# Splitting weights further ahead around the stage turns of a decoder trunk, with later normalized slices

## The chip, the cores and the metric

The program runs on one core of a Trainium2 chip. The metric is the device time of one execution in microseconds, from three executions of the kernel before (median, lowest, highest). The profile is of one execution of its own. The engines are TensorE (PE; its weight loads are PEld), VectorE (DVE), ScalarE (ACT), GpSimd (POOL) and SyncE (SP, which issues the weight loads from memory).

## The reference

Two layers over x of 256 tokens by 1024. Each layer is a half-step SwiGLU FFN, a parallel mixer of three causal parts over one input projection, and a second half-step FFN. Each of the three is followed by a residual add and a layer norm.

```python
def swiglu_half(x, w1, w3, w2):
    return 0.5 * ((jax.nn.silu(x @ w1) * (x @ w3)) @ w2)
...
for l in range(DEPTH):
    x = layer_norm(ALPHA * x + swiglu_half(x, ffn1_w1[l], ffn1_w3[l], ffn1_w2[l]), ln1_g[l], ln1_b[l])
    h = x @ w_in[l]
...
    mix = jnp.concatenate([out_a, out_b, out_c], axis=-1) @ w_out[l]
    x = layer_norm(ALPHA * x + mix, ln2_g[l], ln2_b[l])
    x = layer_norm(ALPHA * x + swiglu_half(x, ffn2_w1[l], ffn2_w3[l], ffn2_w2[l]), ln3_g[l], ln3_b[l])
```

out_a is a chunked spatial gating, out_b a gated DeltaNet with eight heads, out_c a gated linear attention with four. The FFN is 2816 wide.

## The kernel before, in words

**Precision by splitting.** x lies transposed in SBUF, features on partitions, as eight slices of 128 x 256. A product of f32 accuracy is three matmuls in fp32r (`mm3`, L224): each weight and each operand is split into a high half, rounded by ScalarE (L199, L232), and a low half, which VectorE gets by a subtraction (L200, L233). The three products are high by high, high by low, low by high.

**Units.** The weights are packed on the host into units of 128 x 1024 in the order in which they are used: `NU` = 167 a layer (66 for the first FFN, 35 for the mixer, 66 for the second FFN). `load` (L176) has SP fetch units into `NRAW` = 5 raw buffers, `conv` (L184) splits one unit into a pair wh, wl out of `NW` = 5 buffers and asks for a later load, and `done` (L212) runs when a unit has been used: it calls `conv` until `LOOK` = 2 further units stand split. A few units of the mixer (`WHOLE`) are used unsplit.

**Order.** The code is traced in program order. A scheduler at compile time then lays each engine's instructions into one fixed order, by priority among those whose inputs and buffers are ready in its own model. `ahead(n)` (L136) gives the instructions in it the priority of code n instructions earlier. At run time each engine follows its fixed order. `mx` tiles with one tag share one buffer, in turn.

**FFN.** `ffn` (L405) goes over 22 tiles of 128 hidden columns. Tile f takes a w1 and a w3 unit (24 matmuls each) into two PSUM banks h1 and h3, `epilogue` (L420) makes silu(h1) * h3 and splits it into gs, and two tiles later a w2 unit adds it into the four banks y that hold the FFN's output; the last two w2 units (four in the last FFN) come together at the end. In the last FFN the w2 product is taken with tokens on partitions, 512 columns per matmul, and tiles of x are transposed in between.

**The turn of a stage.** After an FFN or a mixer, `ln_open` (L327) adds the residual to y slice pair by slice pair (L338), multiplies by the norm's gain and splits the result into xH and xL (L341, L342), before mean and variance are known. The next stage's first matmuls run on this raw x; two extra columns (gain and bias, so 258 instead of 256) let the mean and the bias be put right afterwards: `raw_t` (L390) adds mean times the extra column (L394) and multiplies by 1/sigma (L395). Meanwhile GpSimd sums x over slices (L345 to L355), ScalarE squares it (L349), VectorE sums the squares (L351 to L356), two matmuls with a constant matrix (`ln_mm`, L358) give the means, and `ln_stats` (L363) makes 1/sigma in small steps on ScalarE and VectorE.

An FFN with a norm ahead of it (the second of layer 0, the first and the second of layer 1: three) computes its tiles 0 to 3 (`NORM` = 4) from raw x. Its statistics are traced between the two units of tile 1. Behind tile 1 the normalized x is made in place, `ln_d` and `ln_n` (L378, L382), alternately by VectorE and GpSimd, and behind tile 2 `ln_x` (L386) and eight splits make the pair x2 from which tiles 4 to 21 are computed. Tile 2 uses two of the y banks as h1 and h3. The mixer (L546) does the same with its first nine units; its three first (L647) run interleaved over the slices.

Of the kernel before, what the change touches and what calls it, by code (L numbers as in the profile page):

```python
# [25 lines left out]
KD = 8  # L26
DFF = 2816
XS = T + 8
NORM = 4
NF = DFF // P  # L30
NU = 2 * 3 * NF + 27 + 8
NRAW = 5
# [2 lines left out]
LAG = 2  # L35
PIECES = 1
FIRST = 3
HP0, HP1, HP2, HP7 = 0, 400, 300, 0
CONST = 3
EVAC = 12  # L40
CUTS = ((9, 1), (17, 4), (35, 4))
ORDER = "v0 sub cv a0 tk0 zz av v3 v1 l0a l0b z3 l1a v2 zr l1b tk1 avn tv z1 zm s0 cq s1 d1 d0 dk a1 c0 pp kt t0 sc s2 c1 t1 s3 c2 pz w1 po c3 t2 w3 t3 w0 w2".split()
# [81 lines left out]
def trunk(ctx: ExitStack, tc: tile.TileContext, xin, w_all, cin, pin, lin, gin, out, dbg=None, nlayers=L):  # L124
# [59 lines left out]
    def conv(upto):  # L184
        b = st["conv"]
        if b > min(upto, nunits - 1):
            return
        load(b)
        st["conv"] += 1
        if whole(b):  # L190
            load(b + NRAW + FIRST * (b < FIRST))
            return
        WH[b] = whp.tile([P, 1024], F32R, tag="wh", name=f"wh{b}")
        WL[b] = whp.tile([P, 1024], F32R, tag="wl", name=f"wl{b}")

        i = b % NU - 3 * NF
        w = 1024 // next((c for o, c in CUTS if 0 <= i < o), 1)
        for o in range(0, 1024, w):
            st["copy"] = A.copy(WH[b][:, o:o + w], raw[b][:, o:o + w])  # L199
            V.tensor_sub(WL[b][:, o:o + w], raw[b][:, o:o + w], WH[b][:, o:o + w].bitcast(F32))  # L200
# [11 lines left out]
    def done(b):  # L212
        for d in (WH, WL, raw):
            d.pop(b, None)
        while st["conv"] < nunits and (sum(not whole(u) for u in range(b + 1, st["conv"])) < LOOK):
            conv(st["conv"])

    def next_unit():
# [95 lines left out]
    def unit_tile(h, b, raw_in):  # L314
        w = T + 2 if raw_in else T
        for k in range(KD):
            mm(h, b, k, w)


# [7 lines left out]
    def ln_open(y, scale, l, n):  # L327
        gb = lnc(l, n)
        s2 = mx.tile([P, 2, T], F32, tag="Y", name="s2")
        q2 = mx.tile([P, 2, T], F32, tag="ls", name="q2")  # L330
        sums[:] = [s2, q2]
        with ahead(HP0):
            A.copy(xH[:, :, T:], gb)
            V.tensor_sub(xL[:, :, T:], gb, xH[:, :, T:].bitcast(F32))
            sqp = None
            for i in range(4):
                xs = x[:, 2 * i:2 * i + 2]
                V.scalar_tensor_tensor(xs, xs, scale, y[i].rearrange("p (a t) -> p a t", a=2),  # L338
                                       op0=ALU.mult, op1=ALU.add)
                for k in (2 * i, 2 * i + 1):  # L340
                    A.activation(xH[:, k, :T], x[:, k], AF.Copy, scale=gb[:, k, 0:1])  # L341
                    V.scalar_tensor_tensor(xL[:, k, :T], x[:, k], gb[:, k, 0:1], xH[:, k, :T].bitcast(F32),  # L342
                                           op0=ALU.mult, op1=ALU.subtract)
                if i == 1:
                    G.tensor_tensor(s2, x[:, 0:2], xs, op=ALU.add)  # L345
                elif i > 1:
                    G.tensor_tensor(s2, s2, xs, op=ALU.add)
                sq = wk.tile([P, 2, T], F32, tag="sq", name="sq")
                A.activation(sq, xs, AF.Square)  # L349
                if i == 1:  # L350
                    V.tensor_add(q2, sqp, sq)  # L351
                elif i > 1:
                    V.tensor_add(q2, q2, sq)
                sqp = sq
            G.tensor_tensor(s2[:, 0], s2[:, 0], s2[:, 1], op=ALU.add)  # L355
            V.tensor_add(q2[:, 0], q2[:, 0], q2[:, 1])  # L356

    def ln_mm(ps, which):  # L358
        with ahead(0):
            PE.matmul(ps[:, which * T:(which + 1) * T], lhsT=C("mean"), rhs=sums[which][:, 0],  # L360
                      start=which == 0, stop=True, skip_group_check=True)

    def ln_stats(ps, eps, hp=0):  # L363

        t0 = wk.tile([P, T], F32, tag="t1", name="rs0")
        t1 = wk.tile([P, T], F32, tag="t3", name="rs1")
        with ahead(hp):
# [8 lines left out]
            V.scalar_tensor_tensor(rs, t0, 1.5, rs, op0=ALU.add, op1=ALU.mult)  # L376
# [18 lines left out]
        V.tensor_mul(t, t, rs)  # L395
        return t

    def raw_silu(dst, p, tag="t1"):
        cc = wk.tile([P, 1], F32, tag="cc", name="cc")
        V.tensor_copy(cc, p[:, T + 1:T + 2])  # L400
        t = raw_t(p, tag)
        act(dst, t, AF.Silu, bias=cc)


    def ffn(ln=None, last=None):  # L405
# [14 lines left out]
        def epilogue(f):  # L420
            h1, h3 = hq.pop(f)
            s = wk.tile([P, T], F32, tag="s", name="s")
            g = wk.tile([P, T], F32, tag="g", name="g")
            if ln and f < NORM:
                raw_silu(s, h1)
                t3 = raw_t(h3, "t3")
                V.scalar_tensor_tensor(g, t3, h3[:, T + 1:T + 2], s, op0=ALU.add, op1=ALU.mult)
            else:
                act(s, h1[:, :T], AF.Silu)
                V.tensor_mul(g, s, h3[:, :T])  # L430
            gH, gL = gs[:, 0, f % 4], gs[:, 1, f % 4]
            split(gH, gL, g)
            gq[f] = (gH, gL)

        pst = early = None
        for f in range(NF + LAG):
            if f < NF:
                if ln and f == 2:
# [4 lines left out]
                if f == 0:  # L443
                    w = T + 2 if ln else T
                    hs = [h1, h3]
                    if st["unit"] == 0:
                        early = hbank("h1")
                        hs.append(early)
                    bs = [next_unit() for _ in hs]
                    for k in range(KD):  # L450
                        for h, b in zip(hs, bs):
                            mm(h, b, k, w)
                    for b in bs:
                        done(b)
                else:
                    if early is None:
                        b = next_unit()
                        if ln and f == NORM:

                            PE.matmul(h1, lhsT=WH[b][:, :P], rhs=gs[:, :, (f - 3) % 4], start=True, stop=True,  # L460
                                      skip_group_check=True)
                        unit_tile(h1, b, ln and f < NORM)
                        done(b)
                    early = None
                    if ln and f == 1:
                        pst = ybank(0, "pst")
                        ln_mm(pst, 0)
                        ln_mm(pst, 1)
                        ln_stats(pst, ln[2])
                    b = next_unit()  # L470
                    unit_tile(h3, b, ln and f < NORM)
                    done(b)
                if f == CONST and st["unit"] < NU // 9:

# [7 lines left out]
                    epilogue(0)  # L482
                if not (ln and f == 0):
                    epilogue(f)
                if ln and f == 1:
                    for i in range(4):
# [59 lines left out]
    def mixer(l, n_ln, eps):  # L546
# [107 lines left out]
        for _, b, _, _ in hd:  # L654
            done(b)
        pst = ybank(0, "pst")
        ln_mm(pst, 0)
        ln_mm(pst, 1)
        ln_stats(pst, eps, HP1)
        h, _, t, i = hd[0]  # L660
        with ahead(HP2):
            epi(t, i)(h)
# [639 lines left out]
```

## Time and profile before

| | |
|---|---|
| three executions | 1102.03 us median, 1096.82 to 1108.56 |
| profiled execution | 1108.28 us, span from first to last instruction 1106.5 us |
| mean granted TensorE clock | 0.973 of full speed |
| read from memory | 179.81 MB, 163 GB/s over the span |
| first FFN of layer 0 | about 5 to 189 us |
| mixer of layer 0 | about 189 to 353 us |
| second FFN of layer 0 | about 353 to 542 us (turn 1 at its start) |
| first FFN of layer 1 | about 542 to 736 us (turn 2) |
| mixer of layer 1 | about 736 to 905 us |
| second FFN of layer 1 | about 905 to 1098 us (turn 3) |

A group of the profile reads: line, engine, operation, out<-in, shape, count | busy time, mean duration in ns of one | idle time of the engine just before them, and what ended it. A window gives length, then busy time and count of each engine, the granted clock, the share of the DMA engines and GB/s. A timeline row gives start, duration, engine, line, operation, and in brackets the idle time before it. Durations of neighbours on one engine can overlap a little, and those of matmuls do so much (0.28 us each, one every 0.113 us).

### The profile page before, as it was taken

To read this page: it belongs to the slowest core of one execution; us is meant where nothing else is said; L and a number is where in the kernel's file an instruction comes from. 1 tells how busy PE (TensorE), PEld (TensorE's weight loads), DVE (VectorE), ACT (ScalarE), POOL (GpSimd) and SP (SyncE) were. 2 spreads that over 40 slices of the span, in tenths; PEclk is the share of its full clock that TensorE was granted. 3 is DMA by queue.
4 is the path that set the end of the run, shared out by engine and by line. 5 is a ranking of instruction groups with operands and counts; after the bars stand their busy time and mean duration, and the time that the engine had idled before them with its cause. 6 is when DMAs were issued, how large, how long until landed. Compare 5 with 4: busy or idle time off the path is not lost. (4 is left out here: it accounts for less than half of the span.)

```text
span 1106.5 us, 23698 instructions
## 1 busy us (share of the span) xinstructions
PE 1062.1 (96%) x9875; PEld 1012.5 (92%) x9875; DVE 753.9 (68%) x1262; ACT 600.4 (54%) x1063; POOL 78.6 (7%) x62
## 2 busy tenths in 40 slices
PE   8999999999999899999989999999989998999996
PEld 7999999987889899999889999999787897999995
DVE  4555556989867965555786555579896679655556
ACT  5444445777556744444664444468664567444442
POOL 0100001101002200000220000020000012000000
PEclk9999999999999999999989999999996999999999
DMA  8855554442323375555336656534331234655541
GB/s 275 303 194 193 193 198 161 153 135 77 116 78 123 138 244 191 192 195 198 140 118 225 193 195 198 195 136 162 124 114 62 97 115 154 229 195 191 191 165 39
DMA packets 51515, 182.38 MB, mean 165 GB/s; under 512 B 5840, under 2 KB 7376, under 8 KB 51280
## 3 DMA queue, kind: packets, MB, share of 16 engines
q1 hardware_dynamic: 50544, 177.23, 47.6%
q10 hardware_dynamic: 864, 3.64, 0.9%
q8 instruction: 77, 1.26, 0.4%
q14 instruction: 30, 0.25, 0.1%
HBM read 179.81 MB, written 1.05 MB: 163 GB/s over the span
## 5 line engine op out<-in xcount | busy, mean ns | idle before, releaser
L200 DVE TENSOR_TENSOR wl<-raw,wh 128x1024 fp32r<-128x1024 f32 (+1 forms) x455 | 413.8, 926 | 236.9 <-ACT wh L199 236.6
L199 ACT CAST wh<-raw 128x1024 fp32r<-128x1024 f32 (+1 forms) x455 | 353.2, 800 | 365.8 <-issue 183.1
L227 PE MATMUL h<-x,wh 128*128 128x256 f32 x864 | 238.7, 276 | 0.0
L228 PE MATMUL h<-x,wh 128*128 128x256 f32 x864 | 238.6, 276 | 0.0
L229 PE MATMUL h<-x,wl 128*128 128x256 f32 x864 | 238.6, 276 | 0.0
L228 PEld LDWEIGHTS h<-x,wh 128*128 128x128 f32 x864 | 162.2, 188 | 0.8
L227 PEld LDWEIGHTS h<-x,wh 128*128 128x128 f32 x864 | 162.2, 188 | 0.7
L229 PEld LDWEIGHTS h<-x,wl 128*128 128x128 f32 x864 | 162.2, 188 | 0.0
L227 PE MATMUL y<-gs,wh 128*128 128x256 f32 x528 | 147.0, 279 | 7.2 <-ACT gs L232 7.2
L228 PE MATMUL y<-gs,wh 128*128 128x256 f32 x528 | 147.2, 279 | 0.0
L229 PE MATMUL y<-gs,wl 128*128 128x256 f32 x528 | 147.1, 279 | 0.0
L228 PE MATMUL h<-xL,wh 128*128 128x256 f32 (+1 forms) x472 | 132.9, 282 | 2.3 <-DVE xL L342 2.1
L227 PE MATMUL h<-xH,wh 128*128 128x256 f32 (+1 forms) x472 | 134.0, 284 | 0.8 <-ACT wh L199 0.7
L229 PE MATMUL h<-xH,wl 128*128 128x256 f32 (+1 forms) x472 | 133.2, 282 | 0.5 <-DVE wl L200 0.5
L227 PEld LDWEIGHTS y<-gs,wh 128*128 128x128 f32 x528 | 100.1, 190 | 7.6 <-ACT gs L232 7.6
L228 PEld LDWEIGHTS y<-gs,wh 128*128 128x128 f32 x528 | 100.6, 191 | 0.0
L229 PEld LDWEIGHTS y<-gs,wl 128*128 128x128 f32 x528 | 100.5, 190 | 0.0
L228 PEld LDWEIGHTS h<-xL,wh 128*128 128x128 f32 x472 | 90.5, 192 | 3.2 <-DVE xL L342 2.9
L227 PEld LDWEIGHTS h<-xH,wh 128*128 128x128 f32 x472 | 90.6, 192 | 1.7 <-ACT wh L199 1.2
L229 PEld LDWEIGHTS h<-xH,wl 128*128 128x128 f32 x472 | 90.5, 192 | 1.0 <-DVE wl L200 0.9
L430 DVE TENSOR_TENSOR g<-s,h 128x256 f32<-128x256 f32 x76 | 32.0, 421 | 45.8 <-PE h L229 37.3
L345 POOL TENSOR_TENSOR s<-x 128x512 f32<-128x512 f32 x5 | 7.1, 1416 | 520.7 <-DVE x L338 520.7
(363 smaller groups left out, 1960.9 us busy)
## 6 DMA issues: line engine op xcount, KB each, us to landing
raw<-w_all SPq DMA_DIRECT2D x331, 512.0 KB, 3.7
raw<-w_all SPq DMA_DIRECT2D x12, 128.0 KB, 4.1
pl<-pin ACTq DMA_DIRECT2D x2, 730.5 KB, 7.2
cst<-cin ACTq DMA_DIRECT2D x1, 1026.0 KB, 8.6
x<-xin SPq DMA_DIRECT2D x4, 256.0 KB, 4.2
out<-xT SPq DMA_DIRECT2D x4, 256.0 KB, 2.0
Gb<-gin ACTq DMA_DIRECT2D x1, 512.0 KB, 3.5
Bb<-gin ACTq DMA_DIRECT2D x1, 512.0 KB, 4.0
```

The source lines that it names most:

```text
L199: st["copy"] = A.copy(WH[b][:, o:o + w], raw[b][:, o:o + w])
L200: V.tensor_sub(WL[b][:, o:o + w], raw[b][:, o:o + w], WH[b][:, o:o + w].bitcast(F32))
L227: PE.matmul(o, lhsT=wh, rhs=mh, start=first, stop=False, **kw)
L228: PE.matmul(o, lhsT=wh, rhs=ml, start=False, stop=False, **kw)
L229: PE.matmul(o, lhsT=wl, rhs=mh, start=False, stop=last, **kw)
L345: G.tensor_tensor(s2, x[:, 0:2], xs, op=ALU.add)
L430: V.tensor_mul(g, s, h3[:, :T])
```

## The change

- `done` keeps more than two units split ahead near the end of a stage: up to six (`LOOK` + 4), from 12 units before the turn on, in steps; ahead of a second FFN, which follows a mixer, in the steps of a table over the last eight units.
- For 29 units the pair of halves lies in `mx` buffers that the mixer uses otherwise (`SPARE`, four pairs), so nine pairs are to be had around a turn. The second FFN's first four units use them, elsewhere every second unit from seven before to five behind the turn.
- `NORM` goes from 4 to 7: tiles 0 to 6 are computed from raw x.
- `ln_open` is written out in a new order, runs with `ahead(400)` instead of `ahead(0)`, and sums x on VectorE instead of GpSimd. The statistics of both kinds of stage run with `ahead(400)` (the FFN's had 0), the squares' mean first; in the FFN they are traced in the middle of tile 1's second unit.
- `epilogue` runs with `ahead(200)`; it copies h3's extra column as it did h1's, so that both banks are free after `raw_t`; the copy into the high half must come before the next change of ScalarE's table.
- The normalized x is made in four slices behind tiles 2 to 5, each queued behind that tile's gate, all on VectorE and ScalarE.

```diff
-NORM = 4
+NORM = 7
-HP0, HP1, HP2, HP7 = 0, 400, 300, 0
+HP0, HP1, HP2, HP7 = 400, 400, 300, 0
+HPE = 200
+SPARE = (("U64", "qd"), ("kb", "kd"), ("vb", "XP"), ("XA", "AT"))
+STAGES = sorted(l * NU + o for l in range(L) for o in (0, 3 * NF, 3 * NF + 35))[1:]
...
+    spare = {s + i: SPARE[n % 4] for s in STAGES
+             for n, i in enumerate(range(4) if s % NU == 3 * NF + 35 else range(-7, 6, 2))}
...
-        WH[b] = whp.tile([P, 1024], F32R, tag="wh", name=f"wh{b}")
-        WL[b] = whp.tile([P, 1024], F32R, tag="wl", name=f"wl{b}")
+        if b in spare:
+            WH[b], WL[b] = (mx.tile([P, 1024], F32R, tag=t, name=f"w{t}{b}") for t in spare[b])
+        else:
+            WH[b] = whp.tile([P, 1024], F32R, tag="wh", name=f"wh{b}")
+            WL[b] = whp.tile([P, 1024], F32R, tag="wl", name=f"wl{b}")
...
-        while st["conv"] < nunits and (sum(not whole(u) for u in range(b + 1, st["conv"])) < LOOK):
+        left = next((s - b for s in STAGES if s > b), 99)
+        if (b + left) % NU == 3 * NF + 35:
+            look = LOOK + {8: 1, 7: 1, 6: 1, 5: 2, 4: 3, 3: 4}.get(left, 4 if left < 3 else 0)
+        else:
+            look = LOOK + min(4, max(0, (14 - left) // 2))
+        while st["conv"] < nunits and (sum(not whole(u) for u in range(b + 1, st["conv"])) < look):
             conv(st["conv"])
...
+        def add_x(i):
+            V.tensor_add(s2, x[:, 0:2] if i == 1 else s2, x[:, 2 * i:2 * i + 2])
...
+            z(0)
+            square(0)
+            low(0)
+            z(1)
+            square(1)
+            low(1, 2)
+            z(2)
+            square(2)
+            low(3, 4)
+            z(3)
+            add_q(1)
+            square(3)
+            low(5, 6, 7)
+            add_x(1)
+            add_q(2)
+            add_x(2)
+            add_q(3)
+            add_x(3)
             V.tensor_add(q2[:, 0], q2[:, 0], q2[:, 1])
+            V.tensor_add(s2[:, 0], s2[:, 0], s2[:, 1])
...
-            if ln and f < NORM:
-                raw_silu(s, h1)
-                t3 = raw_t(h3, "t3")
-                V.scalar_tensor_tensor(g, t3, h3[:, T + 1:T + 2], s, op0=ALU.add, op1=ALU.mult)
...
+            with ahead(HPE):
+                if ln and f < NORM:
+
+                    c1 = raw_bias(h1)
+                    t1 = raw_t(h1, "t1")
+                    act(s, t1, AF.Silu, bias=c1)
+                    c3 = raw_bias(h3)
+                    t3 = raw_t(h3, "t3")
+                    st["gate"] = V.scalar_tensor_tensor(g, t3, c3, s, op0=ALU.add, op1=ALU.mult)
...
+                tab["ops"].append(A.copy(gH, g))
+                V.tensor_sub(gL, g, gH.bitcast(F32))
...
-                    unit_tile(h3, b, ln and f < NORM)
+                    unit_tile(h3, b, ln and f < NORM, stats if ln and f == 1 else None)
...
-                if ln and f == 1:
-                    for i in range(4):
-                        ln_d(V if i % 2 else G, i)
-                        ln_n(V if i % 2 else G, i)
-                if ln and f == 2:
-                    for k in range(KD):
-                        ln_x(ln[0], ln[1], k)
-                        split(x2[0][:, k], x2[1][:, k], x[:, k])
+                i = f - NORM + 5
+                if ln and 0 <= i < 4:
+                    with tc.issue_after(st["gate"].ins):
+                        ln_d(V, i)
+                        ln_n(V, i)
+                        for k in (2 * i, 2 * i + 1):
+                            ln_x(ln[0], ln[1], k)
+                            split(x2[0][:, k], x2[1][:, k], x[:, k])
```

More of the change, by code (lines that the diff above doesn't have):

```diff
@@ L312, in mm, with unit_tile @@
             mm3(h[:, :w], b, k, oh[:, k, :w], ol[:, k, :w], k == 0, k == KD - 1)
-    def unit_tile(h, b, raw_in):
+    def unit_tile(h, b, raw_in, mid=None):
         w = T + 2 if raw_in else T
         for k in range(KD):
+            if mid and k == KD // 2:
+                mid()
             mm(h, b, k, w)
@@ L331, in ln_open, with z, square, low @@
         sums[:] = [s2, q2]
+        sq = [q2, None, None, None]
+        def z(i):
+            xs = x[:, 2 * i:2 * i + 2]
+            V.scalar_tensor_tensor(xs, xs, scale, y[i].rearrange("p (a t) -> p a t", a=2),
+                                   op0=ALU.mult, op1=ALU.add)
+            for k in (2 * i, 2 * i + 1):
+                A.activation(xH[:, k, :T], x[:, k], AF.Copy, scale=gb[:, k, 0:1])
+        def square(i):
+            if i:
+                sq[i] = wk.tile([P, 2, T], F32, tag="sq", name="sq")
+            A.activation(sq[i], x[:, 2 * i:2 * i + 2], AF.Square)
+        def low(*ks):
+            for k in ks:
+                V.scalar_tensor_tensor(xL[:, k, :T], x[:, k], gb[:, k, 0:1], xH[:, k, :T].bitcast(F32),
+                                       op0=ALU.mult, op1=ALU.subtract)
+        def add_x(i):
+            V.tensor_add(s2, x[:, 0:2] if i == 1 else s2, x[:, 2 * i:2 * i + 2])
+        def add_q(i):
+            V.tensor_add(q2, q2, sq[i])
         with ahead(HP0):
@@ L334, in ln_open, with ln_stats @@
             V.tensor_sub(xL[:, :, T:], gb, xH[:, :, T:].bitcast(F32))
-            sqp = None
-            for i in range(4):
[L337 to L355, printed above, removed]
+            z(0)
[16 more added lines that the diff above has]
+            add_x(3)
             V.tensor_add(q2[:, 0], q2[:, 0], q2[:, 1])
+            V.tensor_add(s2[:, 0], s2[:, 0], s2[:, 1])
     def ln_mm(ps, which):
-        with ahead(0):
+        with ahead(HP1):
             PE.matmul(ps[:, which * T:(which + 1) * T], lhsT=C("mean"), rhs=sums[which][:, 0],
-                      start=which == 0, stop=True, skip_group_check=True)
-    def ln_stats(ps, eps, hp=0):
+                      start=which == 1, stop=True, skip_group_check=True)
+    def ln_stats(ps, eps):
         t0 = wk.tile([P, T], F32, tag="t1", name="rs0")
         t1 = wk.tile([P, T], F32, tag="t3", name="rs1")
-        with ahead(hp):
+        with ahead(HP1):
             A.copy(muN, ps[:, :T])
@@ L396, in raw_t, with raw_bias @@
         return t
-    def raw_silu(dst, p, tag="t1"):
+    def raw_bias(p):
         cc = wk.tile([P, 1], F32, tag="cc", name="cc")
         V.tensor_copy(cc, p[:, T + 1:T + 2])
-        t = raw_t(p, tag)
-        act(dst, t, AF.Silu, bias=cc)
+        return cc
     def ffn(ln=None, last=None):
@@ L423, in epilogue, with stats @@
             g = wk.tile([P, T], F32, tag="g", name="g")
-            if ln and f < NORM:
-                raw_silu(s, h1)
-                t3 = raw_t(h3, "t3")
[L427 to L432, printed above, removed]
-            gq[f] = (gH, gL)
-        pst = early = None
+            with ahead(HPE):
[6 more added lines that the diff above has]
+                    st["gate"] = V.scalar_tensor_tensor(g, t3, c3, s, op0=ALU.add, op1=ALU.mult)
+                else:
+                    act(s, h1[:, :T], AF.Silu)
+                    V.tensor_mul(g, s, h3[:, :T])
+                gH, gL = gs[:, 0, f % 4], gs[:, 1, f % 4]
+                tab["ops"].append(A.copy(gH, g))
+                V.tensor_sub(gL, g, gH.bitcast(F32))
+            gq[f] = (gH, gL)
+        def stats():
+            pst = ybank(0, "pst")
+            ln_mm(pst, 1)
+            ln_mm(pst, 0)
+            ln_stats(pst, ln[2])
+        early = None
         for f in range(NF + LAG):
@@ L464, in ffn @@
                     early = None
-                    if ln and f == 1:
[L466 to L469, printed above, removed]
                     b = next_unit()
-                    unit_tile(h3, b, ln and f < NORM)
+                    unit_tile(h3, b, ln and f < NORM, stats if ln and f == 1 else None)
                     done(b)
@@ L484, in ffn @@
                     epilogue(f)
-                if ln and f == 1:
-                    for i in range(4):
-                        ln_d(V if i % 2 else G, i)
-                        ln_n(V if i % 2 else G, i)
-                if ln and f == 2:
-                    for k in range(KD):
-                        ln_x(ln[0], ln[1], k)
-                        split(x2[0][:, k], x2[1][:, k], x[:, k])
+                i = f - NORM + 5
[3 more added lines that the diff above has]
+                        ln_n(V, i)
+                        for k in (2 * i, 2 * i + 1):
+                            ln_x(ln[0], ln[1], k)
+                            split(x2[0][:, k], x2[1][:, k], x[:, k])
             if f >= LAG:
@@ L656, in mixer @@
         pst = ybank(0, "pst")
+        ln_mm(pst, 1)
         ln_mm(pst, 0)
-        ln_mm(pst, 1)
-        ln_stats(pst, eps, HP1)
+        ln_stats(pst, eps)
         h, _, t, i = hd[0]
```

## The prediction

> **Bound now.** I read the page's busy shares first, then the span cut into windows, then what TensorE waited for, and last the groups and the order of VectorE's work around one stage turn. In the page the number after the percent sign is the count of instructions.
>
> ```profile
> PE 1062.1 (96%) x9875; PEld 1012.5 (92%) x9875; DVE 753.9 (68%) x1262; ACT 600.4 (54%) x1063; POOL 78.6 (7%) x62
> ```
>
> TensorE is busy nearly throughout, so only what keeps its matmuls from following each other can be won. Busy time hides that: a slow matmul is busy too. So I count matmuls by window (each row: length, busy time and count per engine, granted clock, DMA share, GB/s).
>
> ```profile
> 353.00:385.00 32.00, 27.31 (x207) 26.56 (x206) 32.00 (x54) 23.47 (x42) 10.47 (x7) 0.95 0.38 132
> 542.00:584.00 42.00, 36.54 (x257) 35.28 (x256) 39.03 (x67) 27.60 (x50) 12.12 (x8) 0.88 0.30 104
> 905.00:946.00 41.00, 36.33 (x259) 34.09 (x258) 40.70 (x67) 28.77 (x48) 10.29 (x7) 0.96 0.45 147
> 385.00:540.00 155.00, 155.00 (x1367) 154.96 (x1366) 89.25 (x106) 73.21 (x98) 0.00 (x0) 1.00 0.59 201
> 189.00:240.00 51.00, 49.83 (x430) 45.74 (x428) 48.60 (x105) 39.13 (x95) 4.94 (x3) 1.00 0.44 145
> 240.00:353.00 113.00, 107.04 (x1466) 94.55 (x1466) 87.66 (x215) 67.73 (x155) 12.90 (x12) 0.94 0.29 97
> 400.00:520.00 120.00, 120.00 (x1061) 120.00 (x1060) 65.29 (x74) 55.03 (x74) 0.00 (x0) 1.00 0.58 195
> 560.02:565.78 5.76, 5.76 (x50) 5.76 (x49) 5.76 (x9) 4.08 (x5) 2.67 (x2) 1.00 0.22 78
> ...
> L521 PE MATMUL y<-wh,gs 128*128 128x512 f32 x8 | 3.8, 474 | 0.0
> ```
>
> In the middle of an FFN (400 to 520) a 256-wide matmul goes by every 120/1061 = 0.113 us, and VectorE is busy little over half the time. A 258-wide matmul of a raw tile takes 5.76/48 = 0.120 (two units of 24; the row's 50 counts a neighbour at each edge). The first three rows are the three FFNs that open on a raw input. Charged wholly at the dearer 0.120, turn 1 needs 207 x 0.120 = 24.8 of its 32 us: 7.2 lost. Turn 2: 257 x 0.120 = 30.8 of 42: 11.2 lost. Turn 3 holds 24 matmuls with 512 columns (three lines like the last row, eight each), charged twice 0.113: 235 x 0.120 + 24 x 0.227 = 33.6 of 41: 7.4 lost. Together 25.8 us, all with VectorE at 93 to 100%.
>
> ```profile
> PE y L227 <- ACT gs L232: 7.2, 2, 4.1
> ...
> PE y L520 <- ACT gs L232: 4.1, 1, 4.1
> PE h L228 <- DVE xL L342: 2.1, 1, 2.1
> ...
> PE pmisc L228 <- DVE xL L342: 1.9, 2, 1.0
> ```
>
> TensorE's waits (total, times, longest) name the same places: the first w2 unit waits for the gated product of tile 0 once in each turn, 11.3 us, and the openings wait for the low halves of x. The 113 us of the mixer's middle are a chain of small steps; the change does not touch its steps.
>
> **VectorE's lateness.** These are its groups, two of GpSimd's, and single instructions, from the second turn.
>
> ```profile
> L200 DVE TENSOR_TENSOR wl<-raw,wh 128x1024 fp32r<-128x1024 f32 x11 | 13.4, 1218 | 2.0 <-ACT wh L199 2.0
> L342 DVE SCALAR_TENSOR_TENSOR xL<-x,lnp,xH 128x256 fp32r<-128x256 f32 x8 | 7.1, 921 | 0.0
> L395 DVE TENSOR_TENSOR t<-t,rs 128x256 f32<-128x256 f32 x8 | 5.3, 688 | 0.0
> L233 DVE TENSOR_TENSOR x<-x,x 128x256 fp32r<-128x256 f32 x8 | 3.1, 421 | 0.0
> L394 DVE SCALAR_TENSOR_TENSOR t<-muN,h 128x256 f32<-128x256 f32 x6 | 2.9, 477 | 1.2 <-PE h L229 1.2
> L380 DVE TENSOR_TENSOR x<-x,muN 128x512 f32<-128x512 f32 x2 | 2.4, 1224 | 0.0
> L427 DVE SCALAR_TENSOR_TENSOR g<-t,h,s 128x256 f32<-128x256 f32 x3 | 1.4, 481 | 0.0
> L400 DVE COPY cc<-h 128x1 f32<-128x1 f32 x3 | 0.5, 154 | 0.9 <-PE h L229 0.9
> ...
> L347 POOL TENSOR_TENSOR s<-s,x 128x512 f32<-128x512 f32 x2 | 4.1, 2032 | 3.5 <-DVE x L338 3.5
> L384 POOL TENSOR_TENSOR x<-x,rs 128x512 f32<-128x512 f32 x2 | 3.6, 1800 | 3.1 <-DVE rs L376 3.1
> ...
> 543.44 1.38 POOL L347 TENSOR_TENSOR s<-s,x 128x512 f32<-128x512 f32 x1 [1.05 <-DVE x L338]
> 543.58 1.51 DVE L342 SCALAR_TENSOR_TENSOR xL<-x,lnp,xH 128x256 fp32r<-128x256 f32 x1
> 545.02 0.68 DVE L351 TENSOR_TENSOR q<-sq 128x512 f32<-128x512 f32 x1
> 545.62 0.87 DVE L342 SCALAR_TENSOR_TENSOR xL<-x,lnp,xH 128x256 fp32r<-128x256 f32 x2
> 546.42 0.67 DVE L338 SCALAR_TENSOR_TENSOR x<-x,y 128x512 f32<-128x512 f32 x1
> 547.01 1.21 DVE L200 TENSOR_TENSOR wl<-raw,wh 128x1024 fp32r<-128x1024 f32 x1
> 548.15 0.68 DVE L353 TENSOR_TENSOR q<-q,sq 128x512 f32<-128x512 f32 x1
> ```
>
> Two things are to be seen. Splits of weights stand between the steps of the normalization. And the same L342 takes 1.51 us beside a GpSimd add and 0.40 (two in 0.80) without one. I also read from these starts that VectorE begins its next instruction about 0.08 us before the last one's end: L338 passes in 0.59, a split in 1.14.
>
> **The parts.**
>
> Two more windows are needed here: the busiest of a turn for the loads, and the mixer's last matmuls.
>
> ```profile
> 367.00:372.75 5.75, 5.75 (x51) 5.75 (x49) 5.75 (x10) 4.12 (x5) 2.65 (x3) 1.00 0.74 280
> 340.00:353.00 13.00, 13.00 (x113) 13.00 (x112) 8.35 (x14) 5.60 (x13) 4.85 (x6) 1.00 0.45 165
> ```
>
> *Splits ahead.* Four more units per turn are split before it: 4 x 1.14 = 4.6 us of VectorE leave each turn. Ahead of turn 2 and of both mixers they fall into the FFN's end, with VectorE idle 42% of the row 385 to 540. Twelve units instead of eight are then split in the last 22 us, 12 x 1.14 + 2.7 tiles x 0.7 = 15.6 us of VectorE: hidden. Their loads come earlier on SP's queue: 12 x 0.524 MB (128x1024 f32) in 22 us would be 286 GB/s, about the 280 that the first of the two windows moved, and five raw units are loaded in advance.
>
> Ahead of turns 1 and 3 they fall into the mixer's last matmuls: 13.0 - 8.35 = 4.7 us idle on VectorE there, against 4.6 wanted. It just fits; where it does not, a split is put into the mixer's last chain. I take 1.5 us lost for both layers (bounds 0, and four splits in the chain of each, 9).
>
> *The opening (five times).* GpSimd's sums move to VectorE: three adds at 0.60 and one at 0.34, +2.1. In return the eight L342 go from 7.1 to 8 x 0.40 = 3.2. Net -1.8 each. And it is placed ahead of the splits, so TensorE's first k-slices find their halves. By the wait rows that is 2.1 in turn 2 (inside the 25.8) and 1.9 at the mixers. The mixer's first 51 us show VectorE at 95% with TensorE nearly full, so freeing VectorE earns little more there: I take 2.5 for both mixers (bounds -3, and 5).
>
> *Statistics.* Both column sums need the opening's adds. VectorE's work after the last y bank is 0.59 + 3 x 0.40 + 6 x 0.60 + 2 x 0.34 = 6.1 us; the mean matmuls now stand in the middle of tile 1's second unit, 48 x 0.120 + 36 x 0.120 = 10.1 us after the turn. They wait for nothing. The means are four f32 matmuls, counted at 0.227 each, 0.9. The chain to 1/sigma is nine small steps at about 0.45, say 5 us; then one multiply, Silu, gate, copy and subtract at about 0.45 each for tile 0: product ready near 10.1 + 0.9 + 5 + 2.3 = 18.3. TensorE reaches that w2 unit after six raw units and the means, 6 x 2.88 + 0.9 = 18.2. So the 4 us wait becomes about none; I allow 0.5.
>
> *Three more raw tiles.* Matmuls: 3 x 48 x 0.007 = 1.0 us per FFN, 3.0 in all, fully on the path. VectorE: one raw epilogue is 2 copies, 2 L394, 2 multiplies, gate, subtract = 0.31 + 0.95 + 0.84 + 0.48 + 0.42 = 3.0, against 0.84 for a plain one.
>
> *Slices behind tiles 2 to 5.* Each is two 512-wide ops and two subtracts, 1.36 + 0.84 = 2.2, all on VectorE; before, all four lay in tiles 1 and 2, half of them on GpSimd at 1.7 to 1.8 us each, which held up L380 (1224 for 680) and L395 (688 for 421). A tile of 3 splits, a raw epilogue and a slice costs 3.66 + 3.0 + 2.2 = 8.86 us by durations, 7.7 with 0.08 off each of its 15 instructions. TensorE gives it 48 x 0.120 + 24 x 0.113 = 8.5. So VectorE is 91% full over tiles 3 to 5, or 4% over, and the four units of lead (4.6 us) cover the latter. The normalized x is due at tile 7 and done behind tile 5: one tile, 8.5 us, of cover. ScalarE has 3 splits x 1.0 and small steps, under 6 of 8.5.
>
> What is left of the loss per turn: 0.5 at the first w2 unit and about 1.0 of small waits in tiles 2 to 6, 1.5, so 4.5 in all. Bounds: 0, and 5 per turn should VectorE be late by durations and by one ScalarE wait per tile.
>
> **The sum.** 25.8 - 3.0 - 4.5 + 2.5 - 1.5 = 19.3 us off the profiled execution, 1108.28 (its span 1106.5 and 1.8 around it): 1089.0. That execution is 6.3 above the median, 1102.03; taken off the median it is 1082.7. Part of the turns' loss is the clock, which may have been worse in that slow execution, so I say 1084.
>
> **The clock.** These matmuls of turn 2 follow a stall and go by every 0.21 us instead of 0.12.
>
> ```profile
> 551.94 0.42 PE L229 MATMUL h<-xH,wl 128*128 128x258 f32 x1
> 552.15 0.42 PE L227 MATMUL h<-xH,wh 128*128 128x258 f32 x1
> ```
>
> The Trainium skill, TensorE: Matmul & The Clock Gate, section Why this matters for your kernels, wants no idle gaps above about 3 us between bursts, else the clock falls to half. The trace agrees, with the granted clock at 0.95, 0.88 and 0.96 in the turns and 1.00 between them. By that rule the clock's share goes with the stalls, and the sum stands.
>
> By the rows alone the share is 0.05 x 32 + 0.12 x 42 + 0.04 x 41 = 8.3 us, the most that a clock which stays low would keep.
>
> **The rivals.**
> - *The mixers gain as well.* Their chain starts earlier and loses clock less: 0.06 x 113 = 6.8 us of the window 240 to 353 is clock. With half of that in each layer and half the residue in the turns: 1102 - 19.3 - 6.8 - 2.3 = 1074. Against: the chain's own steps are unchanged.
> - *VectorE stays the bound through tiles 2 to 6.* For: 8.86 by durations. With 5 us left per turn: 25.8 - 3.0 - 15 + 1 = 8.8 gained, 1093. Against: the 0.08 overlap is plain in the rows.
> - *The change does not do what it says, or the clock stays.* The raw buffers remain five; if splits wait for loads, or the clock's 8.3 us stay, the gain is 19.3 - 8.3 = 11 less a little: 1092. Against: 280 GB/s was moved in a turn.
> - *Slower: VectorE's order idles on ScalarE in each raw tile.* The gate waits for Silu, the subtract for its copy, two subtracts for normalize-and-copy: about 3.0 us per tile of 0.6 to 1.2 each. Then a tile takes 8.86 + 3.0 = 11.9 against 8.5; 3.4 x 5 tiles x 3 turns = 51, less 13.8 of lead, plus 3.0 raw width = 40 against the 25.8 removed: 1116. It decides from 2.0 us of idle per tile. Against: VectorE was busy 39.03 of 42 in turn 2, so ready splits fill such holes.
>
> **The numbers.** 0.58 for the forecast (own range 1076 to 1090), 0.12 for 1074, 0.17 for 1093, 0.05 for 1092, 0.08 for 1116. About what a measurement of this kernel can tell from no change is 1%, 11 us. Faster by over 1% (below 1091): 0.58 + 0.12 = 0.70. Within 1%: 0.17 + 0.05 = 0.22. Slower: 0.08. The range 1071 to 1098 holds the first four cases, less their tails, and leaves out the last.
>
> **Signs.** Right: windows of the three turns at 1.5 us of loss each, granted clock 1.00 in them; no wait of y on gs above 1 us; L342 at about 0.47 mean; GpSimd almost unused; 258-wide matmuls risen by 432. Wrong: VectorE idle on ScalarE inside tiles 2 to 6, h waiting for wh or wl there, or the mixer's last chain longer with 128x1024 splits inside it. The forecast falls if the turns still lose over 4 us each.

## The result, and the profile after

The changed kernel takes 1070.15 us (median of four, 1067.48 to 1072.10), the kernel before beside it 1105.3 (four, 1096.82 to 1109.08): a ratio of 0.9706, interval 0.9655 to 0.9757. Every ratio below is likewise to the kernel before, run beside the variant. Against the median that was shown, 1102.03, it gains 31.9 us; 18 were forecast, and 1070.15 lies 0.85 below the low end of the range.

From the page after, the span and the busy time of each engine:

```profile
span 1070.3 us, 23745 instructions
PE 1045.3 (98%) x9875; PEld 999.5 (93%) x9875; DVE 761.2 (71%) x1360; ACT 602.7 (56%) x1063; POOL 30.4 (3%) x30
```

GpSimd keeps 30 of its 62 instructions. VectorE's busy time grows by 7.3 us only, though it has 98 instructions more: the ones that it had grew shorter. The three turns and the two mixers in windows, after:

```profile
348.00:380.00 32.00, 31.92 (x264) 31.64 (x263) 29.59 (x61) 19.47 (x32) 0.00 (x0) 1.00 0.42 146
532.00:574.00 42.00, 41.97 (x349) 41.69 (x348) 39.52 (x82) 26.37 (x47) 0.00 (x0) 1.00 0.38 128
875.00:916.00 41.00, 40.93 (x305) 39.15 (x304) 38.41 (x76) 25.70 (x42) 0.00 (x0) 1.00 0.56 180
...
190.00:348.00 158.00, 151.83 (x1902) 136.30 (x1901) 135.81 (x326) 108.08 (x252) 11.58 (x10) 0.99 0.35 116
717.00:875.00 158.00, 153.26 (x1899) 137.09 (x1897) 135.28 (x325) 107.45 (x252) 9.52 (x6) 0.98 0.34 111
```

In the three turns 264, 349 and 305 matmuls pass where 207, 257 and 259 did, at clock 1.00. Charged as the prediction charged them, 264 x 0.120 leaves 0.3 us lost in turn 1, 349 x 0.120 leaves 0.1 in turn 2, and turn 3 holds 36 matmuls with 512 columns now, three lines of twelve like this one:

```profile
L568 PE MATMUL y<-wh,gs 128*128 128x512 f32 x12 | 4.7, 394 | 0.0
```

So 269 x 0.120 + 36 x 0.227 = 40.5 leaves 0.5 in turn 3: 0.9 us in all, instead of 25.8. The kernel before's mixers in the same view:

```profile
189.00:353.00 164.00, 156.87 (x1893) 140.28 (x1892) 136.25 (x319) 106.86 (x250) 17.84 (x15) 0.96 0.34 112
736.00:905.00 169.00, 160.22 (x1896) 143.59 (x1895) 136.62 (x319) 107.39 (x251) 14.91 (x11) 0.93 0.33 111
```

The mixers pass as many matmuls in 158 and 158 us as before in 164 and 169; the clock rose from 0.96 and 0.93 to 0.99 and 0.98. TensorE's largest waits inside the program after (total, times, longest), where before 11.3 us stood on the gated product:

```profile
PE p2a L904 <- issue: 3.6, 2, 2.1
PE pv L244 <- DVE wl L210: 2.0, 2, 1.5
```

Both lines belong to the mixer; no wait is left in the turns. Stage by stage, each from its own first matmul to the next stage's first, and the last one to the end of its last matmul, in us:

| profiled execution | FFN1, layer 0 | mixer 0 | FFN2, layer 0 (turn 1) | FFN1, layer 1 (turn 2) | mixer 1 | FFN2, layer 1 (turn 3) |
|---|---|---|---|---|---|---|
| before | 183.8 | 164.8 | 189.2 | 193.3 | 169.5 | 192.3 |
| before, a second look | 184.2 | 161.6 | 189.2 | 191.8 | 160.7 | 192.6 |
| after | 185.1 | 157.8 | 184.5 | 184.5 | 158.3 | 186.2 |
| after, a second look | 185.0 | 157.7 | 184.5 | 184.5 | 156.2 | 186.2 |

The 36.2 us between the first and the third row's spans (1106.5 and 1070.3) are 4.7 + 8.8 + 6.1 = 19.6 in the FFNs with a turn, 7.0 + 11.2 = 18.2 in the mixers, less 1.3 given back in the first FFN and 0.3 at the two ends. The 1.3 go with the lead: at the usual pace the first FFN takes 185.0 to 185.4 in the profiles with it, 183.8 to 184.3 in those without.

### The profile page after: what moved, and what is told of

Read it like the earlier page. It is cut to its first block, busy times and chain, and to the rows that moved or that the text cites. A ratio compares the mean times of both kernels' runs of the same rounds, so it can differ in the third digit from the quotient of the medians.

```text
span 1070.3 us, 23745 instructions
## 1 busy us (share of the span) xinstructions
PE 1045.3 (98%) x9875; PEld 999.5 (93%) x9875; DVE 761.2 (71%) x1360; ACT 602.7 (56%) x1063; POOL 30.4 (3%) x30
## 4 chain that ended last, share of the span: by engine, by line
PE 90%; DVE 5%; ACT 2%; DMA 1%; issue 1%; DVEq 0%; SPq 0%; ACTq 0%
PE h L242 14%; PE h L244 14%; PE h L243 14%; PE y L244 6%; PE y L242 6%; PE y L243 6%; PE y L570 2%; PE y L569 2%; PE y L568 2%; PE yo L243 1%; PE yo L242 1%; PE yo L244 1%; DVE wl L210 1%; PE h L323 1%; DMA raw<-w_all 1%
## 5 line engine op out<-in xcount | busy, mean ns | idle before, releaser
L210 DVE TENSOR_TENSOR wl<-raw,wh 128x1024 fp32r<-128x1024 f32 (+1 forms) x426 | 373.9, 895 | 178.6 <-ACT wh L209 178.3
L209 ACT CAST wh<-raw 128x1024 fp32r<-128x1024 f32 (+1 forms) x426 | 322.1, 783 | 281.1 <-issue 124.9
L242 PE MATMUL h<-x,wh 128*128 128x256 f32 x688 | 190.1, 276 | 0.0
L243 PE MATMUL h<-x,wh 128*128 128x256 f32 x688 | 190.1, 276 | 0.0
L244 PE MATMUL h<-x,wl 128*128 128x256 f32 x688 | 190.1, 276 | 0.0
L244 PE MATMUL y<-gs,wl 128*128 128x256 f32 x480 | 133.1, 277 | 0.0
L242 PE MATMUL y<-gs,wh 128*128 128x256 f32 x480 | 133.1, 277 | 0.0
L243 PE MATMUL y<-gs,wh 128*128 128x256 f32 x480 | 133.1, 277 | 0.0
L243 PEld LDWEIGHTS h<-x,wh 128*128 128x128 f32 x688 | 129.2, 188 | 0.7
L242 PEld LDWEIGHTS h<-x,wh 128*128 128x128 f32 x688 | 129.2, 188 | 0.6
L244 PEld LDWEIGHTS h<-x,wl 128*128 128x128 f32 x688 | 129.2, 188 | 0.0
L243 PEld LDWEIGHTS y<-gs,wh 128*128 128x128 f32 x480 | 90.4, 188 | 0.0
L242 PEld LDWEIGHTS y<-gs,wh 128*128 128x128 f32 x480 | 90.2, 188 | 0.0
L478 ACT CAST gs<-g 128x256 fp32r<-128x256 f32 x88 | 35.3, 401 | 27.6 <-DVE g L472 21.1
```

Source lines behind the costliest of these rows:

```text
L242: PE.matmul(o, lhsT=wh, rhs=mh, start=first, stop=False, **kw)
L243: PE.matmul(o, lhsT=wh, rhs=ml, start=False, stop=False, **kw)
L244: PE.matmul(o, lhsT=wl, rhs=mh, start=False, stop=last, **kw)
L478: tab["ops"].append(A.copy(gH, g))
```

## The experiments

Variants of the kernel after begin with a, of the kernel before with b. Where a median and a profile disagree, the stage lengths say why: in some executions TensorE runs a whole FFN slower (last section), some 6.5 us each time. Such an FFN is called a slow one below.

**Without the lead** (a_nolead): splits stay two ahead and five pairs of halves are used, all else as after.

```diff
-    spare = {s + i: SPARE[n % 4] for s in STAGES ...
+    spare = {}
...
-        left = ...
+        look = LOOK
```

> The changed kernel with the lead undone: two units ahead everywhere, five pairs of buffers, all else as changed. Theory (the lead relieves VectorE in the turns and, by the same relief, the mixers run shorter): the three FFN turns lose about 4 us each again and the mixers give back most of their 17 us, so about 1095 us. Rival (the mixers gained by another part, by GpSimd leaving the opening or by the priorities): only the turns lose, about 1082 us.

Measured: 1077.11 (1072.65 to 1080.33, four), ratio 0.975 (0.9691 to 0.9808). Its turns:

```profile
355.00:387.00 32.00, 31.94 (x262) 31.53 (x261) 31.75 (x63) 22.71 (x34) 0.00 (x0) 1.00 0.59 185
539.00:581.00 42.00, 41.80 (x346) 41.37 (x345) 41.56 (x85) 28.66 (x46) 0.00 (x0) 1.00 0.52 166
883.00:924.00 41.00, 41.00 (x305) 39.23 (x304) 40.73 (x81) 29.90 (x47) 0.00 (x0) 1.00 0.60 193
```

VectorE is now full (31.75 of 32), yet TensorE passes 262, 346 and 305 matmuls against 264, 349 and 305. Given the rest of the change, the lead doesn't clear the turns: without it the FFNs with a turn take 183.9, 183.9 and 186.2 us, beside 184.5, 184.5 and 186.2. Of its profile's 8.2 us over after, about 6 are one slow FFN and 3.6 the mixers (159.2 and 160.5): that is where the lead shows.

**Four raw tiles again** (a_norm4, and a_norm4_again in a later session): slices 0 and 1 behind tile 1, 2 and 3 behind tile 2, still on VectorE.

```diff
-NORM = 7
+NORM = 4
...
-                i = f - NORM + 5
+                for i in {1: (0, 1), 2: (2, 3)}.get(f, ()) if ln else ():
```

> The changed kernel with four raw tiles again: normalized slices 0 and 1 behind tile 1, slices 2 and 3 behind tile 2, all on VectorE, all else as changed. Theory (VectorE's work has to be spread over the tiles behind a turn): 3.0 us of 258-wide matmuls are saved, about 3 us of waits come back in each FFN turn, 1076 us. Rival (the lead alone suffices and three more raw tiles are only a cost): 1067 us.

> The changed kernel with four raw tiles once more, beside the changed kernel in the same session. If the raw tiles are only a cost once VectorE is not held up: 1066 to 1069 us in executions without an FFN at the slow pace, 2 to 4 us below the changed kernel. If the spread over tiles 2 to 5 is needed: 1074 us again, with waits in the turns.

Measured: 1074.67 (1072.12 to 1075.64, four), ratio 0.9727 (0.9675 to 0.9778); again 1072.73 (1066.11 to 1079.64, six), 0.9741 (0.9676 to 0.9806). The first profile has one slow FFN (188.8), the second none; the second's FFNs with a turn take 183.5, 183.8 and 185.2 against 184.5, 184.5 and 186.2 after: 2.7 us less. So the three further raw tiles cost what the prediction charged, 3.0, and pay nothing for it. The medians don't show it, since executions of either spread by more; 1066.11 is the lowest time of any execution in this study.

**The sums back on GpSimd** (a_gsum), the rest as after:

```diff
-            V.tensor_add(s2, x[:, 0:2] if i == 1 else s2, x[:, 2 * i:2 * i + 2])
+            G.tensor_tensor(s2, x[:, 0:2] if i == 1 else s2, x[:, 2 * i:2 * i + 2], op=ALU.add)
...
-            V.tensor_add(s2[:, 0], s2[:, 0], s2[:, 1])
+            G.tensor_tensor(s2[:, 0], s2[:, 0], s2[:, 1], op=ALU.add)
```

> The changed kernel with the column sums of x on GpSimd again in the opening, all else as changed. Theory (VectorE has slack after the lead, so L342's slowing beside GpSimd is hidden): mean of L342 back near 0.9 us, time 1070 to 1074 us. Rival (GpSimd leaving the opening is what cleared the turns and the mixers): 1080 us or more.

Measured: 1097.96 (1093.98 to 1107.92, ten), ratio 0.9964 (0.9923 to 1.0005). One small edit gives back nearly the whole gain, though it also shifts the scheduler's order in places; the junk adds below don't. The low halves in the groups, and TensorE's waits:

```profile
L365 DVE SCALAR_TENSOR_TENSOR xL<-x,lnp,xH 128x256 fp32r<-128x256 f32 x40 | 30.9, 812 | 3.5 <-ACT xH L356 3.5
```

```profile
PE pst L401 <- DVE q L396: 7.7, 3, 3.1
...
PE pst L401 <- issue: 3.0, 1, 3.0
```

The low halves take 812 ns instead of 480, the sums come late, and TensorE stops at the mean matmuls (pst), which its fixed order now has early. The FFNs with a turn are 3.9, 3.8 and 2.4 us longer than after, the mixers 6.5 and 4.9: 21.5 of the 21.9 between the spans.

**Priorities as before** (a_noprio): opening, epilogue and the FFN's statistics at the old priorities.

```diff
-HP0, HP1, HP2, HP7 = 400, 400, 300, 0
+HP0, HP1, HP2, HP7 = 0, 400, 300, 0
-HPE = 200
+HPE = 0
...
-        with ahead(HP1):
+        with ahead(hp):
...
```

> The changed kernel with the priorities of before: opening and FFN statistics at 0, epilogues at 0, the mixer's statistics at 400 as in both kernels. Theory (with units split ahead nothing competes with the opening, so priority matters little): 1071 to 1076 us. Rival (the priorities set the order that shortened the mixers): 1085 us or more, the mixers back at 165 to 169 us each.

Measured: 1083.51 (1079.58 to 1085.47), ratio 0.9799 (0.9735 to 0.9862). This looked like a cost of 13 us, but the profile puts it elsewhere: the FFNs with a turn take 184.8, 184.8 and 186.0, as after; the first FFN is a slow one (191.5), and the two mixers differ, though TensorE, VectorE and ScalarE have the same order in both:

```profile
196.00:352.00 156.00, 151.54 (x1903) 135.61 (x1902) 136.28 (x326) 108.28 (x252) 10.05 (x10) 0.99 0.37 118
722.00:889.00 167.00, 160.37 (x1899) 143.56 (x1898) 136.25 (x325) 107.87 (x251) 7.78 (x6) 0.93 0.33 105
```

The second is 11.5 us longer at clock 0.93. The lower clock isn't that one execution's: the four here have mean clocks of 0.985 to 0.990, those of after 0.993 to 0.995. That points to the old priorities, though four executions don't settle it, and for the slow first FFN nothing tells. The turns don't need the priorities.

**The kernel before, GpSimd's work to VectorE** (b_vec: sums and normalization; b_vecsum: the sums alone).

```diff
-            G.tensor_tensor(s2, x[:, 0:2], xs, op=ALU.add)
+            V.tensor_tensor(s2, x[:, 0:2], xs, op=ALU.add)
...
-                    ln_d(V if i % 2 else G, i)
+                    ln_d(V, i)
-                    ln_n(V if i % 2 else G, i)
+                    ln_n(V, i)
```

> The kernel before with one edit: the column sums and the normalization's subtract and multiply run on VectorE where GpSimd had them; order, lead, priorities and raw tiles as before. New theory (GpSimd beside VectorE is what made the turns late, and the lead, the spread and the priorities add little): about 1080 us, FFN turns at half of their loss or less. Rival (all parts are needed together; VectorE, with more to do and no lead, stays the bound): 1095 us or more.

> The kernel before with only the three column sums and their fold on VectorE; the normalization stays half on GpSimd. New theory (the sums beside L342 are the costly part): most of what the run with all of GpSimd's work moved gains, 1083 us. Rival (GpSimd's share of the normalization, 1.7 to 1.8 us each, is the costly part): 1095 us or more.

Measured: b_vec 1084.68 (1080.84 to 1095.88, four), ratio 0.9855 (0.9783 to 0.9926); b_vecsum 1104.77 (1096.73 to 1111.21, ten), 1.0022 (0.9988 to 1.0057). The turns of b_vec:

```profile
350.00:382.00 32.00, 31.66 (x257) 30.99 (x256) 31.95 (x65) 25.09 (x45) 0.00 (x0) 1.00 0.43 145
533.00:575.00 42.00, 39.04 (x314) 37.82 (x313) 41.20 (x80) 30.77 (x53) 0.00 (x0) 1.00 0.43 148
885.00:926.00 41.00, 40.94 (x305) 39.05 (x305) 39.88 (x75) 30.30 (x51) 0.00 (x0) 1.00 0.51 177
```

Five moved lines bring turns 1 and 3 to 257 and 305 matmuls, and turn 2, which opens a slow FFN, to 314 of 349. The FFNs with a turn take 183.3, 192.5 (the slow one) and 185.6 us. VectorE has more to do and gets through more: 65, 80 and 75 instructions, against 54, 67 and 67 in the same lengths before. With the sums alone moved, TensorE still waits for the gated product:

```profile
PE y L227 <- ACT gs L232: 6.2, 2, 3.2
...
PE y L520 <- ACT gs L232: 2.9, 1, 2.9
```

So the normalization on GpSimd matters as well as the sums. In the profiled execution of b_vecsum three FFNs were slow ones (190.6, 192.7 and 193.4), some 19 of its 1099.9 us. The other nine executions have no profile, and none is below 1096.73; so what the edit is worth by itself stays open.

**The kernel before with the lead alone** (b_lead): the table, the nine pairs and the steps of the diff's first half, nothing else.

```diff
+    spare = {s + i: SPARE[n % 4] for s in STAGES ...
...
-        while st["conv"] < nunits and (sum(...) < LOOK):
+        while st["conv"] < nunits and (sum(...) < look):
```

> The kernel before with only the lead: up to six units ahead in nine pairs of buffers. The prediction's theory (4.6 us of VectorE leaves each turn): the turns lose 3 to 4 us each less, 1088 us. New theory (the lead alone leaves the collision with GpSimd in place): 1095 to 1102 us.

Measured: 1090.03 (1088.10 to 1092.52), ratio 0.9888 (0.9845 to 0.993). Its turn 2:

```profile
535.00:577.00 42.00, 37.12 (x275) 35.98 (x275) 36.65 (x66) 24.56 (x45) 11.05 (x7) 0.92 0.26 86
```

275 matmuls against 257 (270 in the second look at before), but far from 349, and VectorE is now idle for over 5 us of the 42. The FFNs with a turn take 186.9, 192.0 and 190.2, beside 189.2, 191.8 and 192.6 in the second look at before, the mixers 157.8 and 160.6, beside 161.6 and 160.7. Splits out of the way aren't enough while GpSimd is at work.

**GpSimd busy for nothing** (a_gjunk): after, with three more adds on GpSimd in each opening, whose sums nobody reads; VectorE keeps its own.

```diff
+            if i:
+                G.tensor_tensor(junk, x[:, 0:2], xs, op=ALU.add)
...
+        junk = mx.tile([P, 2, T], F32, tag="va", name="junk")
```

> The changed kernel, in which GpSimd also adds the same slices of x in the opening into a buffer that nobody reads; VectorE's own sums stay, so nothing waits for GpSimd. If GpSimd harms by holding up VectorE: L365 back near 0.8 us mean and 1085 us or more. If it harms only because its sums come late: 1070 to 1074 us.

Measured: 1096.31 (1090.91 to 1099.68, ten), ratio 0.9946 (0.9914 to 0.9978), 26 us above after. Its groups, GpSimd's third add around turn 2, VectorE there (start, duration), and TensorE's largest wait in the openings:

```profile
L367 DVE SCALAR_TENSOR_TENSOR xL<-x,lnp,xH 128x256 fp32r<-128x256 f32 x40 | 29.9, 788 | 1.2 <-ACT xH L356 1.2
...
L358 POOL TENSOR_TENSOR junk<-x 128x512 f32<-128x512 f32 x15 | 23.8, 1590 | 568.1 <-DVE x L353 568.1
```

```profile
548.65 1.37 POOL L358 TENSOR_TENSOR junk<-x 128x512 f32<-128x512 f32 x1 [1.05 <-DVE x L353]
```

```profile
548.81 1.77 DVE L376 TENSOR_TENSOR q<-q,sq 128x512 f32<-128x512 f32 x1
...
552.29 0.68 DVE L376 TENSOR_TENSOR q<-q,sq 128x512 f32<-128x512 f32 x1
```

```profile
PE pst L405 <- DVE q L400: 10.3, 4, 3.1
```

Nothing waits for these 15 adds, 23.8 us of GpSimd in all. VectorE's add that begins 0.16 us behind GpSimd's takes 1.77 and ends 0.56 after it; alone it takes 0.68. It made next to no way while GpSimd ran. The junk adds apart, all engines run the same instructions in the same order as after (9875 matmuls, 1360 instructions of VectorE, 1063 of ScalarE), so no change of order brings the waits at pst that after doesn't have; the lateness by itself does. Of the 25.6 us between the two spans 6.3 are a slow first FFN; the five stages with an opening make up some 20, 13.4 of them the waits at pst.

**Lead and VectorE together on the kernel before** (b_lead_vec): the edits of b_lead and b_vec; order, priorities, four raw tiles and the slices of before.

> The kernel before with two edits: GpSimd's sums and its half of the normalization on VectorE, and the lead of up to six units in nine pairs of buffers; four raw tiles, the old opening and priorities. Theory (these two hold nearly all of the gain; three more raw tiles, the slices and the priorities add nothing that can be measured): 1067 to 1074 us, level with the changed kernel. Rival (the new order, the priorities and seven raw tiles are needed): 1080 us or more.

Measured: 1074.32 (1069.62 to 1080.63, six), ratio 0.9754 (0.9693 to 0.9816). Its turns:

```profile
354.00:386.00 32.00, 32.00 (x263) 31.59 (x263) 30.18 (x64) 23.15 (x43) 0.00 (x0) 1.00 0.31 99
537.00:579.00 42.00, 42.00 (x351) 41.63 (x351) 38.77 (x78) 28.06 (x51) 0.00 (x0) 1.00 0.38 125
880.00:921.00 41.00, 41.00 (x311) 39.31 (x310) 37.71 (x72) 27.30 (x48) 0.00 (x0) 1.00 0.49 165
```

The turns are as clear as after (more of their matmuls are the 256-wide ones). The FFNs with a turn take 183.4, 183.4 and 184.9 us, 3.5 less than after's, which the three raw tiles would explain; the mixers take 158.4 and 159.1, 1.4 more than in the first look at after and 3.6 more than in the second. The span, 1073.6, holds a slow first FFN (190.6); less some 6.5 it is 1067, beside 1068.1 of the second look at after. Its median lies 3.5 us above the second look's, with overlapping intervals: within what these runs can tell, two edits carry the whole change.

**Both kernels once more** (after_again, before_again), unedited, the second for its profile:

> The changed kernel once more, for the spread of its executions and for TensorE's pace in its four FFNs: 1067 to 1073 us, a 256-wide matmul every 0.113 us in each of them if the slow pace (0.118) comes after disturbed stretches only; one or more FFNs at 0.118, and executions near 1077, if the pace falls by chance alone.

> The kernel before once more, for a second profile. If its mixers were long in the first profile because of that execution's clock: mixers of 158 to 162 us and a span near 1098. If its own order makes them long: 164 us or more in each again.

Measured: after 1070.87 (1069.45 to 1085.79, six), ratio 0.9712 (0.9655 to 0.977); before, one execution, 1095.85. This look at before met a better clock than the first (0.985 against 0.973):

```profile
351.00:383.00 32.00, 27.30 (x207) 26.54 (x207) 32.00 (x55) 23.46 (x41) 9.84 (x6) 0.95 0.39 132
540.00:582.00 42.00, 36.55 (x270) 35.29 (x269) 40.16 (x69) 27.76 (x49) 11.72 (x7) 0.92 0.34 109
892.00:933.00 41.00, 36.32 (x255) 34.17 (x255) 40.32 (x67) 28.40 (x49) 10.51 (x7) 0.92 0.44 144
...
189.00:351.00 162.00, 153.80 (x1904) 137.77 (x1903) 137.26 (x320) 108.01 (x253) 18.25 (x15) 0.98 0.35 114
732.00:892.00 160.00, 151.99 (x1894) 135.86 (x1893) 135.96 (x319) 107.19 (x251) 14.75 (x11) 0.99 0.37 117
```

The turns are nearly as bad as in the first look; the mixers' clock is 0.98 and 0.99 instead of 0.96 and 0.93, and they take 161.6 and 160.7 us. Between the two second looks, with like clocks in the mixers, the FFNs with a turn gain 4.7 + 7.3 + 6.4 = 18.4 and the mixers 3.9 + 4.5 = 8.4.

## Why the prediction came out as it did

**The turns: right, in size and in the wait that went.** 25.8 - 3.0 - 4.5 = 18.3 us were to come from the three FFNs; 19.6 and 18.4 came in the two pairs of profiles. The residue is smaller than the 1.5 us a turn forecast (0.9 in all), the clock in them is 1.00, and no wait of y on gs is left. The clock did go with the stalls, as the rule on idle gaps has it in the Trainium skill, TensorE: Matmul & The Clock Gate, section Why this matters for your kernels; the rival in which the clock stays low is out. By the timeline of VectorE around turn 2, which begins at 532.4:

```profile
537.85 0.68 DVE L369 TENSOR_TENSOR s<-s,x 128x512 f32<-128x512 f32 x1
538.45 0.41 DVE L396 TENSOR_TENSOR q<-q 128x256 f32<-128x256 f32 x1
538.78 0.41 DVE L397 TENSOR_TENSOR s<-s 128x256 f32<-128x256 f32 x1
...
545.45 0.43 DVE L417 SCALAR_TENSOR_TENSOR rs<-rs,rs 128x256 f32<-128x256 f32 x1
```

The sums are done 6.8 us into the turn (6.1 after the last bank were forecast) and 1/sigma at 13.5 (10.1 + 0.9 + 5 = 16), so tile 0's product is in time.

**VectorE's single prices: right.** The groups after, by form (the last two within turn 2):

```profile
L365 DVE SCALAR_TENSOR_TENSOR xL<-x,lnp,xH 128x256 fp32r<-128x256 f32 x40 | 17.5, 480 | 1.2 <-ACT xH L356 1.2
...
L436 DVE TENSOR_TENSOR t<-t,rs 128x256 f32<-128x256 f32 x10 | 4.1, 422 | 0.1
L421 DVE TENSOR_TENSOR x<-x,muN 128x512 f32<-128x512 f32 x3 | 2.1, 686 | 0.0
```

The low halves fell from 888 (the mean of all 40 before) to 480 against 0.47 forecast; the operations that GpSimd held up fell from 688 to 422 and from 1224 to 686. VectorE is busy 39.52 of turn 2's 42 us and TensorE doesn't wait: the rivals with VectorE as the bound, through its work or through idle time on ScalarE, are out.

**Wrong: the term for the mixers, by its size and by its parts.** "I take 2.5 for both mixers (bounds -3, and 5)", less "1.5 us lost for both layers" for the lead, made 1.0. The mixers gained 8.4 at like clocks (6.2 against the first look at after) and 18.2 in the first pair. The step that failed is "the change does not touch its steps", said of the chain in the mixer's middle: its steps stayed, but what TensorE waits for between them did not. Three waits of TensorE on VectorE stand in the mixers before and are gone after, 10.3 us together:

```profile
PE p1a L850 <- DVE iv L833: 4.7, 2, 2.8
...
PE pau L227 <- DVE XP L932: 3.7, 2, 1.9
...
PE pmisc L228 <- DVE xL L342: 1.9, 2, 1.0
...
PE pst L360 <- DVE q L356: 0.4, 2, 0.2
```

One wait grew, p2a on issue, from 1.7 to 3.6. The runs tell which part removes which. The first stands, at 4.6 or 4.7, in every profile without the lead (both looks at before, b_vec, b_vecsum, a_nolead) and in none with it. In a_nolead it and the second are:

```profile
PE p1a L893 <- DVE iv L876: 4.6, 2, 2.3
...
PE pau L237 <- DVE XP L975: 3.7, 2, 1.9
```

The second goes only by the lead and the new priorities together: it stands in a_nolead, a_noprio, b_lead and b_lead_vec. The third is gone in b_vec, where GpSimd has left the opening. Against the second look at before, the mixers of b_vec are 2.8 us shorter, those of b_lead 3.9 and those of b_lead_vec 4.8, one profile each. So b_vec roughly bears out the opening's 2.5, and the lead, charged with a loss, gave a gain. How the lead makes VectorE's steps of the chain come in time wasn't looked at.

In the new order the openings hold a larger price. A GpSimd add doesn't just stretch the low half beside it: it delays every step queued behind. After the change the mean matmuls stand early in TensorE's fixed order, so TensorE stops there: the junk adds cost some 20 us in five openings with no data waiting for them, the returned sums 21.9. In the kernel before the wait at pst is the 0.4 us above, and GpSimd's harm lies in the turns, in the gated product.

**Wrong: the weight of the lead.** "4 x 1.14 = 4.6 us of VectorE leave each turn" was the cover of the whole step. It isn't needed for the turns: a_nolead clears them without it, and b_vec's, its slow FFN taken as 6.5 us, gain 18.7 with neither lead nor further raw tiles. So the forecast's 18.3 came out through GpSimd's leaving, more than through the lead. On the kernel before, where GpSimd still holds VectorE up, it is worth 7.8 us of span (1094.1 to 1086.3), and the moves to VectorE 15.0 (1094.1 to 1079.1) with a slow FFN in it, so about 21. Together they reach after. The three raw tiles cost 2.7 to 3.5; the slices, the order and the priorities add nothing to the turns, and in the mixers the 1.4 to 3.6 us by which after is ahead of b_lead_vec.

**The rest of the distance is the clock.** The rival "The mixers gain as well", 1074, came closest; it had a chance of 0.12, and both things that it asked for came, shorter mixers that lose less clock and half the residue or less. The profile of before that the sum was made against had its clock low in the mixers for longer than after, about 10 of the 18.2 us; the prediction took 6.3 off for that execution but gave the change nothing for the mixers' clock. Part of this is chance: the second look at before has 0.98 and 0.99 there as well. Part points to the change. Over whole executions the mean clock was 0.992 to 0.995 in nine of the changed kernel's ten and 0.985 in the tenth; in the 43 of the kernel before beside the other runs it was 0.982 to 0.988 in 22 and 0.967 to 0.980 in 21. Clean turns account for 8.3 us by the prediction's sum, some 0.008 of this, which lifts 0.985 to 0.993. Means some hundredth below a kernel's best came in half the executions before and in one of ten after; ten are few, so the share of the change in it stays open.

## What to carry to other kernels

An engine that does side work in its idle time isn't free if its reads hold up the engine that everything queues on: look for the same instruction with two durations (here 0.40 and 1.51 us), see what ran beside the long one, and price the lateness of the whole queue behind it, not the stretched instruction alone. Dummy work that nothing reads measures such a hold-up by itself. And before crediting a large change with its gain, build its smallest edits alone on the old kernel: here two of them, put together, can't be told from the whole.

## What the runs showed of the hardware

**GpSimd stops VectorE rather than sharing with it.** The 1.77 us add above ended 0.56 us after GpSimd's. The Trainium skill, SBUF — State Buffer, section Who interferes with whom, says that a VectorE instruction with two SBUF inputs contends with a GpSimd instruction that reads SBUF; this case agrees, at 0.68 against 1.77 us. That side work of 23.8 us costs this program some 20 us is the runs' own number.

**Two paces of TensorE at one clock.** A stretch of an FFN from 60 to 180 us, after and then without the lead:

```profile
60.00:180.00 120.00, 120.00 (x1058) 120.00 (x1057) 68.97 (x78) 58.85 (x79) 0.00 (x0) 1.00 0.63 211
```

```profile
60.00:180.00 120.00, 120.00 (x1021) 120.00 (x1021) 62.54 (x71) 53.30 (x72) 0.00 (x0) 1.00 0.58 186
```

Both show clock 1.00 and a full TensorE, but a matmul every 120/1058 = 0.113 us and every 120/1021 = 0.118. The slower pace holds for a whole FFN, some 6.5 us, and was seen in 9 of the 42 first three FFNs of 14 profiles, never in those of the two unedited kernels. What sets it wasn't found.

**Half clock in a mixer.** The two mixers of a_noprio, 156 and 167 us, have the same order on TensorE, VectorE and ScalarE; the second spent 17 us on end at half clock:

```profile
816.00:833.00 17.00, 17.00 (x196) 14.91 (x196) 8.23 (x22) 7.05 (x16) 0.00 (x0) 0.50 0.14 52
```

With its shorter stretches the row's 0.93 makes 0.07 x 167 = 11.7 us of clock, about the difference. The two profiles of before differ by 12 us, nearly all in the mixers with the lower clock, which is why single totals here say less than stage lengths.
